# Block transposes on VectorE for a scan's inputs and outputs, with block layouts in DRAM, and another order of the lanes

## The chip, the cores and the metric

The kernel runs on 1 core of one Trainium2 chip. The metric is the device time of one execution in microseconds; runs of one kernel are compared by their median. One execution is also profiled, and that is the trace read here.

## The reference

One layer of a bidirectional hybrid encoder, for a group of 256 tokens ("prompt") and one of 1024 ("sample") with the same weights. Width 2048.

```
hn   = rms_norm(x);  proj = hn @ w_in
xbc, z_ssd, dt_raw, q, k, v, z_att, mq, z_mem = split(proj)
xbc  = silu(centred_dwconv(xbc, conv_w, conv_b))        # 5 taps along the tokens, 1536 channels
xs, B, C = split(xbc, (1024, 256, 256))
y    = ssd_scan(forward) + ssd_scan(backward) + d_skip * xs       # chunks of 128 tokens, 16 heads of 64
o_ssd = rms_norm(y * silu(z_ssd), per group of 512 channels)
o_att = window_attention(q, k, v, sink) * silu(z_att)
o_mem = memory_attention(mq, rms_norm(mem) @ w_mem_kv) * silu(z_mem)
out  = x + concat[o_ssd, o_att, o_mem] @ w_out
```

All in float32. Each large product is made of three float32r matmuls, with both operands split into a high and a low part (names that end in H and L, or wh and wl).

## The kernel before, in words

The 1280 tokens are ten tiles of 128: 0 to 7 are the sample, 8 and 9 the prompt, and they are worked in two groups of five tiles (640 tokens). There are two kinds of weight stage. `block_tok` makes 512 output columns for up to five token tiles, with 16 steps over the input features (three matmuls a tile and step). `block_pair` makes the feature-major outputs (channels on the partitions, tokens along the row) with seven products in place of eight; each unit has 8 steps, GpSimd makes the weight sums (`ws`), ScalarE and VectorE split them (`wh`, `sh`, `wl`, `sl`).

In order of time: the memory's keys and values; `q` for group 1; `seven_stage(1)` (100 to 380 us) with the feature-major part of `w_in` (gates, and the 12 blocks `fc` of 128 convolution channels); `kv` and `q`; `seven_stage(0)` (460 to 714 us); then the token-major stages of `w_in` from 714 us on, beside which the scan and both attentions run; then `w_out`, token-major first (1272 to 1550 us) and by pairs last.

**The convolution.** `conv_work` takes a finished block `u` of 128 channels x 642 columns through five taps and a SiLU, and its `last` stores it in DRAM in `xbc_d`, rows of channels by columns of tokens. Blocks 0 to 7 are x, 8 to 11 are B and C. Its pieces stand in the queue `left` and are taken out a piece at a time between the weight steps.

**The lanes.** In the later stages, what isn't a weight matmul is written as generators in four lanes: ATT (`attn`, `mem_attn`), SSD (`ssd_one`, `ssd_two`), PREP (heads' norms and transposes) and DEC (`decay`). After each weight step `pump` gives every lane some credit and takes steps from lanes that may run. A step yields `wants(tiles, banks, after)`: a small clock model (`Clocks`) holds it back until its tiles should be ready and, if it needs PSUM, until a bank should be free; with `banks` over 0 the tiles must be ready, otherwise they may be 300 ns away. `said` holds what is done. `pump` asks the lanes in a fixed order. `need` and `settle` take steps by force where a later stage can't go on without them: `refill_o(0)` wants `attn` 4, `mem_attn` 4 and `ssd_two` 5.

**The scan.** `ssd_one(t)` goes through the sample's tiles downward from 7 to 0 and then 9 and 8. It loads x, B and C of its tile from `xbc_d`, turns x so that tokens stand on the partitions (`pxs`, four 128x128 transposes on TensorE for each half of 512 channels), copies it out of PSUM (`xs`), and makes the chunk states. `decay(t)` makes the part within the chunk and stores `yp_d`. `ssd_two(t)` goes upward, adds the other direction, multiplies by the gate and takes the norm. The finished y of a tile is turned back one tile later by `turn_ssd`: four transposes on TensorE (`pr`), a copy by ScalarE (`so`), and a store to `oT_d[2 + g]`, where channels stand on the rows and a group's 640 tokens along them.

**Who reads `oT_d`.** `refill_o(0)` loads group 0's outputs as the rows of the token-major `w_out` stages (`fill_direct`, tile `chd`); `seven_load` loads group 1's for the stage by pairs (`raw`, profile names `ra` and `rb_`).

All these DMAs are issued by SyncE, in one queue, with the weight loads (`wraw`).

Of the kernel before, what the change touches and what calls it, by code (L numbers as in the profile page):

```python
# [19 lines left out]
P = 128  # L20
D = 2048
KT = D // P
NT = 10
# [122 lines left out]
def wants(*tiles, banks=0, after=()):  # L146
    return tiles, banks, after
# [3 lines left out]
def hymba_encoder_kernel(  # L151
# [67 lines left out]
    def dram(shape, name):  # L219
        return dr.tile(shape, F32, tag=name, name=name)  # L220

    xbc_d = dram([12, P, NT * P], "xbc_d")
    z_d = [[dram([P, 512], f"z{c}_{t}") for t in range(NT)] for c in range(2)]
    zT_d = [[dram([P, 4, 640], f"zT{c}_{g}") for g in range(2)] for c in range(2)]
    q_d = [dram([P, 512], f"q_{t}") for t in range(NT)]
    mq_d = [dram([P, 512], f"mq_{t}") for t in range(NT)]
    kv_d = [dram([P, 288], f"kv_{t}") for t in range(NT)]
    oT_d = [[dram([P, 4, 640], f"oT{c}_{g}") for g in range(2)] for c in range(4)]
    yp_d = [dram([P, 1024], f"yp_{t}") for t in range(NT)]
    sb_d = [dram([P, 1024], f"sb_{t}") for t in range(NT)]  # L230
    row_d = [[dram([P, 640], f"row{n}{k}") for n in "HL"] for k in range(KT)]
# [1 line left out]
    ac_d = [dram([160, P], f"ac_{g}") for g in range(2)]  # L233
    mr_d = [dram([P, 512], f"mr_{i}") for i in range(4)]
    mv_d = dram([P, 4, 512], "mv_d")

    def turned(out, x):

# [62 lines left out]
    def pump(rates):  # L301

        for i in range(4):
            owed[i] = min(owed[i] + rates[i % 2], DEBT) if lanes[i] else 0.0
        while True:
            i = next((j for j in (ATT, PREP, SSD, DEC) if may(j)), None)
            if i is None:
                return
            owed[i] -= 1
            step(i)  # L310
# [10 lines left out]
    def fill_direct(q, j, src, gain=None, n=640, norm=False):  # L321

        ch = rp.tile([P, 640], F32, tag="ch", name="chd", bufs=CH)[:, :n]
        last_load[0] = S.dma_start(ch, src)
        yield
        h, l = [x[:, :n] for x in new_place(4 * q + j)]
        if norm:
            V.scalar_tensor_tensor(out=ch, in0=ch, scalar=gain, in1=rbc, op0=ALU.mult, op1=ALU.mult)
            gain = None
        if gain is None:  # L330
            A.activation(h, ch, AF.Copy)
            V.tensor_sub(l, ch, h.bitcast(F32))
        else:
            A.activation(h, ch, AF.Copy, scale=gain)
            V.scalar_tensor_tensor(out=l, in0=ch, scalar=gain, in1=h.bitcast(F32), op0=ALU.mult, op1=ALU.subtract)
        yield
# [96 lines left out]
    def conv_work(grp, fc, u):  # L433

        n = 642
        cw = [vec[:, R_CW + k * 12 + fc:R_CW + k * 12 + fc + 1] for k in range(5)]
        c = []

        def first_tap():
            if grp:  # L440
                V.memset(u[:, 384:388], 0.0)
                V.memset(u[:, 644:646], 0.0)
                V.tensor_copy(carry[:, fc, :], u[:, :4])
            else:
                V.memset(u[:, :2], 0.0)
                V.tensor_copy(u[:, 642:646], carry[:, fc, :])
            c.append(ev.tile([P, 650], F32, tag="evt", name="c")[:, :n])
            A.activation(c[0], u[:, :n], AF.Identity, scale=cw[0], bias=vec[:, R_CB + fc:R_CB + fc + 1])

        def tap(k):  # L450
            V.scalar_tensor_tensor(out=c[0], in0=u[:, k:k + n], scalar=cw[k], in1=c[0], op0=ALU.mult, op1=ALU.add)

        def silu():
            A.activation(u[:, :n], c[0], AF.Tanh)

        def last():
            V.scalar_tensor_tensor(out=u[:, :n], in0=u[:, :n], scalar=1.0, in1=c[0], op0=ALU.add, op1=ALU.mult)
            if grp == 0:
                S.dma_start(xbc_d[fc, :, 0:642], u[:, :n])
            else:  # L460
                S.dma_start(xbc_d[fc, :, 642:1024], u[:, :382])
                S.dma_start(xbc_d[fc, :, 1024:1280], u[:, 386:n])
        return [first_tap] + [lambda k=k: tap(k) for k in range(1, 5)] + [silu, last]
# [484 lines left out]
    def ssd_one(t):  # L948
# [5 lines left out]
        xc = []  # L954
        for g in range(2):
            x = wb("xc", shape=(P, 4, P))
            S.dma_start(x, xbc_d[4 * g:4 * g + 4, :, tok].rearrange("f p c -> p f c"))
            xc.append(x)
        yield wants(bc, banks=1, after=prior(t, "weighed"))
        ps = psum("pcb")  # L960
# [10 lines left out]
        said.add(("ssd_one", t, "cb"))  # L971
        xsT = []
        for g in range(2):
            yield wants(xc[g], banks=1, after=prior(t) + (("dt_prep", t // 5 * 5),))
            ps = psum("pxs")
            for j in range(4):
                turned(ps[:, j * P:(j + 1) * P], xc[g][:, j, :])
            xt = mp.tile([P, 512], F32, tag="xs", name="xs", bufs=2)
            V.tensor_copy(xt, ps)
            xsT.append(xt)  # L980
        xs_of[t] = xsT
        yield wants(cb)
# [162 lines left out]
    def turn_ssd(g):  # L1145

        if g in last_y:
            t, y = last_y.pop(g)
            ps = psum("pr")
            for j in range(4):  # L1150
                T.transpose(ps[:, j * P:(j + 1) * P], y[:, j * P:(j + 1) * P], ident)
            o = mp.tile([P, 512], F32, tag="rb", name="so", bufs=RBB)
            A.activation(o, ps, AF.Copy)
            S.dma_start(oT_d[2 + g][t // 5][:, :, t % 5 * P:(t % 5 + 1) * P], hv(o, 4))

    def ssd_two(t):
        first = t in (NS - 1, NT - 1)
        last = t in (0, NS)
        tok = slice(t * P, (t + 1) * P)
        yield wants(after=(("decay", t // NS * NS),))  # L1160
        ss = sm.tile([P, 2], F32, tag="s2", name="yss", bufs=4)
        if not last:
            cc = mp.tile([P, 2, P], F32, tag="btok", name="cc", bufs=1)
            S.dma_start(cc, xbc_d[10:12, :, tok].rearrange("f p c -> p f c"))
        ld = []
        for g in range(2):
            c = slice(g * 512, (g + 1) * 512)

            y = mp.tile([P, 512], F32, tag="ya" if t % 2 else "rf", name="yd", bufs=2)
            S.dma_start(y, yp_d[t][:, c])  # L1170
            z = mp.tile([P, 512], F32, tag="xs", name="zd", bufs=2)
            S.dma_start(z, z_d[g][t])
            st = None
            if not first:
                st = state[:, c] if last else wb("st2")
                S.dma_start(st, sb_d[t][:, c])
            ld.append((y, z, st))
        yield wants(*([last_y["y"][2]] if "y" in last_y else []))
        norm_ssd()
        for g in range(2):  # L1180
            c = slice(g * 512, (g + 1) * 512)
            y, z, st = ld[g]
            yield wants(y, z, *(() if last else (cc, state)), banks=0 if last else 1)
            if not last:
                pf = psum("pyb")
                T.matmul(pf, cc[:, g, :], state[:, c], start=True, stop=True)
                y2 = wb("y3")
                V.tensor_mul(hv(y2), hv(pf), hb(eacs_all[:, t, 8 * g:8 * g + 8], 8, 64))
                V.tensor_add(y, y, y2)
            V.tensor_mul(y, y, z)  # L1190
            if not first and not last:
                V.tensor_mul(hv(state[:, c]), hv(state[:, c]), hb(cd_all[:, t, 8 * g:8 * g + 8], 8, 64))
                V.tensor_add(state[:, c], state[:, c], st)
            yield wants(y)
            A.activation(z, y, AF.Square, scale=0.5, accum_out=ss[:, g:g + 1])
            if g in last_y:
                yield wants(last_y[g][1], banks=1)
                turn_ssd(g)
        yield wants(ss)
        rs = sm.tile([P, 2], F32, tag="s2", name="yrs", bufs=4)  # L1200
        rsqrt(rs, ss, 1.0 / 512, 2)
        G.tensor_scalar(out=rs, in0=rs, scalar1=0.5, scalar2=None, op0=ALU.mult)
        last_y["y"] = t, [x[0] for x in ld], rs
        if first:
            yield wants(rs)
            norm_ssd()
            for g in range(2):
                yield wants(last_y[g][1], banks=1)
                turn_ssd(g)

    seven = {1: (0, 0, 0), 2: (0, 1, 5), 6: (1, 1, 2), 5: (1, 0, 1), 3: (1, 2, 6), 7: (0, 3, 3), 4: (0, 2, 4)}
# [2 lines left out]
    def seven_load(k):  # L1214

        q, j = divmod(k, 4)
        raw[k] = [rp.tile([P, 640], F32, tag="ch", name=n, bufs=CH) for n in ("ra", "rb_")]
        S.dma_start(raw[k][0], oT_d[q][1][:, j, :])
        S.dma_start(raw[k][1], oT_d[2 + q][1][:, j, :])

    def seven_sums(k):
        a, b = raw[k]
# [358 lines left out]
    def refill_o(grp):  # L1581
        def f(q):
            need((attn, mem_attn, ssd_two, ssd_two)[q], [4 if q < 2 else 5])
            return [part(fill_direct, q, j, oT_d[q][grp][:, j, :],
                         gain=None if q < 2 else vec[:, R_SG + 4 * (q - 2) + j:R_SG + 4 * (q - 2) + j + 1])
                    for j in range(4)]
        return f
# [225 lines left out]
    return out  # L1813


W_AT, _o = {}, 0
for _n, _c, _t in _blocks():
    W_AT[_n] = (_o, len(_c), _t)
# [54 lines left out]
```

## Time and profile before

| | |
|---|---|
| three runs | 1776.07, 1778.87, 1780.52 us; median 1778.87 |
| the profiled execution | 1773.83 us, its span 1772.1 us |
| granted TensorE clock | 1.000 |
| tile `pxs` on TensorE | 80 transposes, 782.7 to 1331.8 us |
| tile `pr` on TensorE | 80 transposes, 1161.8 to 1409.9 us |
| DMA, whole span | 313.23 MB in 210993 packets, 21584 of them under 512 B |

Nearly every instruction passes through one helper line (L128), so the groups are told apart by the names of their tiles: `pr<-identr,yd` is what writes `pr` from `identr` and `yd`. PE is TensorE's matmuls, PEld its weight loads, DVE VectorE, ACT ScalarE, POOL GpSimd and SP SyncE. "Idle before" is the time in which the engine stood still ahead of the instructions of a group, and "<-" what ended it. The ends of matmuls are modelled and overlap: what a matmul costs is read from one start to the next.

### The profile page before, as it was taken

To read this page: it belongs to the slowest core of one execution; us is meant where nothing else is said; L and a number is where in the kernel's file an instruction comes from. 1 tells how busy PE (TensorE), PEld (TensorE's weight loads), DVE (VectorE), ACT (ScalarE), POOL (GpSimd) and SP (SyncE) were. 2 spreads that over 40 slices of the span, in tenths; PEclk is the share of its full clock that TensorE was granted. 3 is DMA by queue.
4 is the path that set the end of the run, shared out by engine and by line. 5 is a ranking of instruction groups with operands and counts; after the bars stand their busy time and mean duration, and the time that the engine had idled before them with its cause. 6 is when DMAs were issued, how large, how long until landed. Compare 5 with 4: busy or idle time off the path is not lost.

```text
span 1772.1 us, 30974 instructions
## 1 busy us (share of the span) xinstructions
PE 1755.3 (99%) x10306; PEld 1572.0 (89%) x10306; DVE 1310.9 (74%) x2417; ACT 971.8 (55%) x2181; POOL 683.8 (39%) x1092
## 2 busy tenths in 40 slices
PE   9999999999999999999999999999999999999999
PEld 7889999999899999988788877887788888889999
DVE  5596788989968888797777877678776533766665
ACT  6554555445545444346787666658886532433332
POOL 0026798860478989220110000111200100068775
PEclk9999999999999999999999999999999999999999
DMA  8794454446544333376467766767785734644442
GB/s 293 238 319 175 136 149 148 128 143 194 156 119 145 119 104 106 90 216 208 143 188 249 259 213 192 226 190 230 243 249 161 222 110 147 207 142 147 145 144 77
DMA packets 210993, 313.23 MB, mean 177 GB/s; under 512 B 21584, under 2 KB 84368, under 8 KB 210832
## 3 DMA queue, kind: packets, MB, share of 16 engines
q1 hardware_dynamic: 210688, 311.19, 56.7%
q8 instruction: 81, 1.33, 0.3%
q14 instruction: 80, 0.66, 0.1%
q10 hardware_dynamic: 144, 0.06, 0.0%
HBM read 242.42 MB, written 68.75 MB: 176 GB/s over the span
## 4 chain that ended last, share of the span: by engine, by line
PE 88%; DMA 4%; DVE 3%; ACT 2%; issue 1%; POOL 1%; SPq 0%; ACTq 0%; DVEq 0%; POOLq 0%
PE acc L128 66%; PE accm L128 11%; PE py L128 2%; PE po L128 1%; PE psc L128 1%; PE pst L128 1%; PE pmo L128 1%; PE pms L128 1%; PE ppt L128 1%; DMA wraw<-in_w_in_laid_dram 1%; PE pyf L128 1%; DMA xst<-in_x_prompt_dram 1%; DVE wl L128 1%; PE pyb L128 0%; ACT lg L128 0%
## 5 line engine op out<-in xcount | busy, mean ns | idle before, releaser
L128 PE MATMUL acc<-wh,xH 128*128 128x512 f32 (+1 forms) x1248 | 490.0, 393 | 0.1
L128 DVE TENSOR_TENSOR wl<-wraw,wh 128x512 fp32r<-128x512 f32 (+1 forms) x480 | 355.5, 744 | 172.9 <-ACT wh L128 170.1
L128 PE MATMUL acc<-wl,xH 128*128 128x512 f32 (+1 forms) x1248 | 473.7, 380 | 0.7 <-DVE wl L128 0.5
L128 PE MATMUL acc<-wh,xL 128*128 128x512 f32 (+1 forms) x1248 | 472.1, 378 | 0.0
L128 ACT ACTIVATE wh<-wraw 128x512 fp32r<-128x512 f32 (+1 forms) x480 | 291.5, 613 | 211.6 <-PE acc L128 136.5
L128 POOL TENSOR_TENSOR ws<-wraw 128x128 f32<-128x128 f32 x224 | 156.9, 700 | 365.8 <-DMA wraw<-in_w_in_pairs_dram 163.1
L128 PEld LDWEIGHTS acc<-wl,xH 128*128 128x128 f32 x1248 | 234.7, 188 | 45.1 <-issue 6.5
L128 PEld LDWEIGHTS acc<-wh,xH 128*128 128x128 f32 x1248 | 234.6, 188 | 44.9 <-issue 7.0
L128 PEld LDWEIGHTS acc<-wh,xL 128*128 128x128 f32 x1248 | 234.2, 188 | 44.6 <-issue 1.0
L128 ACT ACTIVATE sh<-ws 128x384 fp32r<-128x384 f32 x224 | 115.5, 522 | 253.3 <-POOL ws L128 126.6
L128 DVE TENSOR_TENSOR sl<-ws,sh 128x384 fp32r<-128x384 f32 x224 | 158.7, 712 | 115.4 <-ACT sh L128 113.9
L128 POOL TENSOR_TENSOR ws<-wraw,ws 128x128 f32<-128x128 f32 x224 | 153.1, 683 | 17.2
L128 POOL TENSOR_TENSOR ws<-ws,wraw 128x128 f32<-128x128 f32 x224 | 154.3, 689 | 0.0
L128 POOL TENSOR_TENSOR wraw<-wraw 128x128 f32<-128x128 f32 x224 | 139.8, 624 | 17.1
L128 PE MATMUL acc<-xH,wl 128*128 128x320 f32 x320 | 100.0, 312 | 1.0 <-DVE wl L128 1.0
L128 PE MATMUL acc<-tH,sl 128*128 128x320 f32 x320 | 98.9, 309 | 0.0
L128 PE MATMUL acc<-xL,wh 128*128 128x320 f32 x320 | 98.9, 309 | 0.0
L128 PE MATMUL accm<-tH,wl 128*128 128x320 f32 x320 | 98.8, 309 | 0.0
L128 PE MATMUL acc<-tH,sh 128*128 128x320 f32 x320 | 98.7, 309 | 0.0
L128 PE MATMUL acc<-xH,wh 128*128 128x320 f32 x320 | 98.7, 309 | 0.0
L128 PE MATMUL accm<-tL,wh 128*128 128x320 f32 x320 | 98.5, 308 | 0.0
L128 PE MATMUL accm<-tH,wh 128*128 128x320 f32 x320 | 98.5, 308 | 0.0
(458 smaller groups left out, 3829.1 us busy)
## 6 DMA issues: line engine op xcount, KB each, us to landing
wraw<-in_w_in_pairs_dram SPq DMA_DIRECT2D x160, 256.0 KB, 2.7
wraw<-in_w_in_laid_dram SPq DMA_DIRECT2D x128, 256.0 KB, 3.6
wraw<-in_w_out_laid_dram SPq DMA_DIRECT2D x64, 256.0 KB, 3.1
wraw<-in_w_out_pairs_dram SPq DMA_DIRECT2D x64, 256.0 KB, 2.9
rf<-ac SPq DMA_DIRECT2D x40, 256.0 KB, 3.8
rb<-ac SPq DMA_DIRECT2D x40, 256.0 KB, 4.2
wraw<-in_w_mem_laid_dram SPq DMA_DIRECT2D x32, 256.0 KB, 4.7
ra<-in_x_turned_dram SPq DMA_DIRECT2D x16, 320.0 KB, 3.8
```

What stands on the lines that cost most here:

```text
L128: r = f(*a, **kw)
```

## The change

- `ssd_one` loads x from a new tensor `x_d`, as blocks of 32 tokens, so that a 32x32 block transpose by VectorE from SBUF to SBUF gives `xs`. The eight transposes on TensorE a tile, their PSUM banks and the copies are gone. 
- A 32x32 block transpose turns within blocks and leaves their places; the places are made good by the layout of `x_d`, by the loads' patterns and by an order of x's channels (`BLOCKED`), by which the columns of `w_in`, the rows of `w_out`, the convolution's weights and the norm's gains are laid out ahead of the launch.
- `conv_work` stores blocks 0 to 7 in `x_d`, in runs of 32 floats, with an extra DMA for the columns at the groups' edge; blocks 8 to 11 go to `xbc_d` as before.
- `turn_ssd` turns y with VectorE's block transpose; TensorE's transposes, the PSUM bank and ScalarE's copy are gone. `oT_d[2]` and `oT_d[3]` are laid out in blocks; `fill_direct` and `seven_load` read them in runs of 32 floats.
- `pump` asks SSD and DEC ahead of ATT and PREP from the time that `mem_attn` 4 is done until `ssd_two` 5 is.

```diff
+    x_d = dram([8, NT * 4, P, 32], "x_d")
...
-    oT_d = [[dram([P, 4, 640], f"oT{c}_{g}") for g in range(2)] for c in range(4)]
+    oT_d = [[dram([P, 4, 640] if c < 2 else [4, 20, P, 32], f"oT{c}_{g}") for g in range(2)] for c in range(4)]
...
+    def blocks(x):
+        return x.rearrange("b p j -> p b j")
+
+    def in_blocks(x):
+        return x.rearrange("p (b j) -> p b j", j=32)
+
+    def turned_blocks(x):
+        return x.rearrange("f a (i q) j -> (a i) f (q j)", q=4)
...
-            i = next((j for j in (ATT, PREP, SSD, DEC) if may(j)), None)
+            late = ("mem_attn", 4) in said and ("ssd_two", 5) not in said
+            i = next((j for j in ((SSD, DEC, ATT, PREP) if late else (ATT, PREP, SSD, DEC)) if may(j)), None)
...
-        last_load[0] = S.dma_start(ch, src)
+        last_load[0] = S.dma_start(in_blocks(ch) if len(src.shape) == 3 else ch, src)
...
-            if grp == 0:
+            if fc < 8:
+                if grp == 0:
+                    S.dma_start(blocks(x_d[fc, 0:20]), in_blocks(u[:, :640]))
+                    S.dma_start(x_d[fc, 20, :, 0:2], u[:, 640:n])
+                else:
+                    S.dma_start(x_d[fc, 20, :, 2:32], u[:, :30])
+                    S.dma_start(blocks(x_d[fc, 21:32]), in_blocks(u[:, 30:382]))
+                    S.dma_start(blocks(x_d[fc, 32:40]), in_blocks(u[:, 386:n]))
+            elif grp == 0:
...
-            S.dma_start(x, xbc_d[4 * g:4 * g + 4, :, tok].rearrange("f p c -> p f c"))
+            S.dma_start(x, turned_blocks(x_d[4 * g:4 * g + 4, 4 * t:4 * t + 4]))
...
-            yield wants(xc[g], banks=1, after=prior(t) + (("dt_prep", t // 5 * 5),))
-            ps = psum("pxs")
-            for j in range(4):
-                turned(ps[:, j * P:(j + 1) * P], xc[g][:, j, :])
+            yield wants(xc[g], after=prior(t) + (("dt_prep", t // 5 * 5),))
             xt = mp.tile([P, 512], F32, tag="xs", name="xs", bufs=2)
-            V.tensor_copy(xt, ps)
+            V.transpose(xt, xc[g].rearrange("p f c -> p (f c)"))
...
-            ps = psum("pr")
-            for j in range(4):
-                T.transpose(ps[:, j * P:(j + 1) * P], y[:, j * P:(j + 1) * P], ident)
             o = mp.tile([P, 512], F32, tag="rb", name="so", bufs=RBB)
-            A.activation(o, ps, AF.Copy)
-            S.dma_start(oT_d[2 + g][t // 5][:, :, t % 5 * P:(t % 5 + 1) * P], hv(o, 4))
+            V.transpose(o, y)
+            S.dma_start(turned_blocks(oT_d[2 + g][t // 5][:, t % 5 * 4:t % 5 * 4 + 4]), hv(o, 4))
...
-                yield wants(last_y[g][1], banks=1)
+                yield wants(last_y[g][1])
...
-        S.dma_start(raw[k][1], oT_d[2 + q][1][:, j, :])
+        S.dma_start(in_blocks(raw[k][1]), blocks(oT_d[2 + q][1][j]))
...
-            return [part(fill_direct, q, j, oT_d[q][grp][:, j, :],
+            return [part(fill_direct, q, j, oT_d[q][grp][:, j, :] if q < 2 else blocks(oT_d[q][grp][j]),
...
+BLOCKED = [128 * f + 32 * q + i for f in range(8) for i in range(32) for q in range(4)]
```

More of the change, by code (lines that the diff above doesn't have):

```diff
@@ L1207, in ssd_two @@
             for g in range(2):
-                yield wants(last_y[g][1], banks=1)
+                yield wants(last_y[g][1])
                 turn_ssd(g)
@@ L1844 @@
     za = _np.arange(C_ZA, C_ZA + 512).reshape(2, 4, 64).transpose(1, 0, 2).reshape(512)
-    c = _np.concatenate([za, _np.arange(C_ZM, C_ZM + 512), _np.arange(C_X, C_X + 1536)]).reshape(10, 256)[list(UNITS)].ravel()
+    c = _np.concatenate([za, _np.arange(C_ZM, C_ZM + 512), C_X + _np.array(BLOCKED), _np.arange(C_X + 1024, C_X + 1536)]).reshape(10, 256)[list(UNITS)].ravel()
     p = w[:, c].reshape(2, 8, P, 10, 2, P)
@@ L1849 @@
     w = _np.asarray(inputs['w_out'])[0]
+    w = _np.concatenate([w[BLOCKED], w[1024:]])
+    inputs['ssd_norm_g'] = _np.asarray(inputs['ssd_norm_g']).ravel()[BLOCKED]
     att = w[1024:1536].reshape(2, 4, 64, D).transpose(1, 0, 2, 3).reshape(512, D)
@@ L1855 @@
     inputs['w_out_pairs'] = _np.stack([w[0, :, :, 0], w[1, :, :, 0], w[1, :, :, 1], w[0, :, :, 1]]).transpose(3, 1, 2, 0, 4).reshape(8, 8, P, 512)
+    for n in ('conv_b', 'conv_w'):
+        inputs[n] = _np.take(_np.asarray(inputs[n]), BLOCKED + list(range(1024, 1536)), axis=-1)
     inputs['vecs'] = _np.concatenate([_np.asarray(inputs[n]).reshape(-1, P) for n in
```

## The prediction

> **What bounds the kernel now.** I read the totals first, then the chain that ended last.
>
> ```profile
> span 1772.1 us, 30974 instructions
> PE 1755.3 (99%) x10306; PEld 1572.0 (89%) x10306; DVE 1310.9 (74%) x2417; ACT 971.8 (55%) x2181; POOL 683.8 (39%) x1092
> ...
> PE 88%; DMA 4%; DVE 3%; ACT 2%; issue 1%; POOL 1%; SPq 0%; ACTq 0%; DVEq 0%; POOLq 0%
> ```
>
> PE is busy for 1755.3 of 1772.1 us and carries 88% of the chain. An instruction taken off PE shortens the span unless what replaces it makes PE wait. VectorE is next, so I cut the span by stage to see where it has room. The columns are the stretch, its length, then the busy time of PE, PEld, DVE, ACT and POOL, the clock, the DMA share and GB/s.
>
> ```profile
> 380.00:460.00 80.00, 80.00 (x500) 74.64 (x499) 73.33 (x127) 39.51 (x72) 16.26 (x17) 1.00 0.56 170
> 460.00:714.00 254.00, 253.71 (x1676) 249.26 (x1675) 213.24 (x312) 123.27 (x228) 208.22 (x311) 1.00 0.41 123
> 760.00:1160.00 400.00, 392.43 (x2136) 321.25 (x2134) 309.16 (x705) 272.81 (x741) 44.83 (x78) 1.00 0.66 207
> 1160.00:1290.00 130.00, 128.38 (x698) 100.34 (x696) 103.83 (x234) 96.20 (x244) 22.39 (x48) 1.00 0.73 226
> 1460.00:1560.00 100.00, 100.00 (x443) 82.80 (x442) 57.39 (x97) 40.33 (x67) 4.59 (x6) 1.00 0.56 169
> ```
>
> The edits to the scan fall in 760 to 1450 us. PE idles there for 7.57 + 1.62 us, no more, and VectorE has room: 77% busy, then 80%. The row of 380 to 460 shows VectorE at 73.33/80 = 92% while PE waits for nothing.
>
> **The transposes that leave PE.** Two groups of four transposes go, each twenty times. A matmul's duration overlaps its neighbour's, so the price is read from starts.
>
> ```profile
> 1400.42 0.39 PE L128 MATMUL acc<-wh,xL 128*128 128x512 f32 x1
> 1400.65 0.60 PE L128 MATMUL pr<-identr,yd 128*128 128x128 f32 x4
> 1401.01 0.48 PE L128 MATMUL acc<-wh,xH 128*128 128x512 f32 x1
> 1401.32 0.39 PE L128 MATMUL acc<-wl,xH 128*128 128x512 f32 x1
> 1401.55 0.39 PE L128 MATMUL acc<-wh,xL 128*128 128x512 f32 x1
> ...
> 1331.35 0.40 PE L128 MATMUL acc<-wh,xH 128*128 128x512 f32 x1
> 1331.59 0.45 PE L128 MATMUL pxs<-identr,xc 128*128 128x128 f32 x4
> 1331.88 0.47 PE L128 MATMUL acc<-wl,xH 128*128 128x512 f32 x1
> 1332.18 0.40 PE L128 MATMUL acc<-wh,xL 128*128 128x512 f32 x1
> ```
>
> Undisturbed, a 512-column matmul starts 0.23 us after the one before (1401.32 to 1401.55). From 1400.42 to 1401.55 stand three of them and one group of pr: 1.13 - 3 x 0.23 = 0.44 us for pr. From 1331.35 to 1332.18 stand two and one group of pxs: 0.83 - 2 x 0.23 = 0.37 us. The counts come from the groups by line:
>
> ```profile
> L128 DVE COPY xs<-pxs 128x512 f32<-128x512 f32 x20 | 13.3, 681 | 0.3 <-PE pxs L128 0.3
> L128 PE MATMUL pr<-identr,yd 128*128 128x128 f32 x80 | 11.9, 275 | 0.3 <-DVE y L128 0.3
> L128 ACT ACTIVATE so<-pr 128x512 f32<-128x512 f32 x20 | 11.6, 592 | 6.7 <-PE pr L128 6.6
> L128 PE MATMUL pxs<-identr,xc 128*128 128x128 f32 x80 | 9.2, 247 | 1.2 <-DMA xc<-xbc_d 0.8 <-DVE nm L128 0.4
> L128 DVE TENSOR_SCALAR yd<-yd,yrs 128x512 f32<-128x512 f32 x20 | 9.0, 483 | 12.5 <-POOL yrs L128 12.5
> L128 DVE RECIPROCAL dtw<-dtw 128x160 f32<-128x160 f32 x6 | 6.9, 1146 | 0.1
> ```
>
> So 20 x 0.44 + 20 x 0.37 = 16.2 us leave PE, about 7.4 us by xs and 8.8 by so. PE's own waits ahead of them (1.2 + 0.3 us) may go too; I count them at zero, because the data still has to come before the next step of the scan, and keep 0 to 1.5 us for the range.
>
> **VectorE takes them over.** The copy of xs out of PSUM (681 ns) becomes a 32x32 block transpose, in its place. The copy of so on ScalarE (592 ns, twenty of them, off the path: 96.20 of 130 us busy) becomes another one on VectorE. No row shows this operation. The nearest is the copy of the same 128x512 elements, 681 ns, and I take it. The ends are the 483 ns of the scaling, and RECIPROCAL's rate: 1146 ns for 160 elements, 3.7 us for 512. At 681 ns xs costs VectorE nothing new and so adds 20 x 0.68 = 13.6 us. By stage, so's rows are (length, ScalarE busy):
>
> ```profile
> 1160.00:1290.00 130.00, 9.35 (x16) 1.00 0.73 226
> ```
>
> Sixteen fall in one stage. There VectorE stands at 103.83 + 10.9 = 114.7 us in a stage of 130 - 16 x 0.44 = 123 us: 93%, against the 92% that PE was seen to bear. I charge 1 us of new waits. VectorE's block of work would make the weights' low part late, and PE behind it.
>
> The Trainium skill, in "VectorE: DVE Perf Modes", section "The three transpose paths", gives 311 ns for a 128x128 VectorE transpose in bf16. Four of them would be 1.24 us (an estimate by that page), by which that stage would gain nothing and the sum would be 14.2 - 7 = 7.2 us; no run shown so far has such an instruction.
>
> VectorE now also waits for the load of xc itself, where PE did. That wait came to 0.8 us in twenty loads, so the loads land ahead of their use, and I charge nothing; behind such a wait stand the weights' splits.
>
> **The smaller pieces in DRAM.** Loads of xc and stores of so keep runs of 512 B (four blocks of 32 floats side by side). Stores of x and loads of oT go from rows to runs of 128 B: 640 columns are 20 x 128 = 2560 pieces, 160 on each of 16 engines. What a piece costs comes from three short stretches of the DMA queue (packets, MB, share of 16 engines): 0.6 us at 783.62 us with loads of 128 B, 1 us at 1403.4 with a store of 512 B, 1 us at 1112.4 with 2 KB.
>
> ```profile
> q1 hardware_dynamic: 220, 0.03, 27.8%
> ...
> q1 hardware_dynamic: 478, 0.24, 89.2%
> ...
> q1 hardware_dynamic: 137, 0.25, 64.7%
> ```
>
> They give 0.278 x 16 x 600/220 = 12.1 ns, 29.9 ns and 75.6 ns a packet (the last mixed with some tiny ones). A blocked transfer then holds the engines for 160 x 12.1 = 1.94 us, where eight rows of 2.5 KB to an engine held them for about 8 x 75.6 x 1.25 = 0.76: 1.2 us more. This happens in three places.
>
> First, 16 stores of x in the two stages of convolution, with 16 more DMAs in all for the edges of 2 and 30 columns. SP has time to issue them, at about half a microsecond each (the stores of oT below, in ns):
>
> ```profile
> SPq L128 <- DVE wl L128: 581.1, 324, 6.8
> ...
> PE acc L128 <- DVE wl L128: 1.5, 4, 0.5
> ...
> L128 SPq DMA_DIRECT2D oT<-so x20: 513/519/1430, 1163.3 to 1412.2; - x20
> L128 SPq DMA_DIRECT2D oT<-moT x10: 518/519/620, 1103.3 to 1446.1; - x10
> L128 SPq DMA_DIRECT2D ra<-oT x8: 320/326/384, 1384.1 to 1541.0; - x8
> ```
>
> It stands 581.1 us waiting for free weight buffers. Weights queued behind a store come 1.2 us late; a step lasts 254/80 = 3.2 us, loads run two steps ahead, and all of PE's waits for split weights are 1.5 us in the whole span. A 128 B store is shown nowhere: I take the load's 12.1 ns, keep 29.9 (a piece of 512 B) as the other end, and charge 1 us for all 16.
>
> Second, eight loads of chd in 1160 to 1290, which may come 1.2 us later, asked for two steps ahead where a step has 15 matmuls of 0.23 us and the lanes' work besides: nothing. Third, eight loads of the last stage:
>
> ```profile
> L128 SPq DMA_DIRECT2D rb__17947<-oT x1: 432/432/432, 1417.4 to 1417.4; - x1
> L128 ACT ACTIVATE rb__17947<-rb__17947,vec x1: 817/817/817, 1492.5 to 1492.5; 128x640 f32<-128x640 f32 x1
> ```
>
> The first is issued 75 us ahead of its use. Later ones are nearer, but PE is busy for 100.00 of 100 us there with ScalarE at 40 and VectorE at 57: nothing.
>
> **The order of the lanes.** From the fifth tile of mem_attn to ssd_two(5) the scan's lanes step ahead of attention. It moves PE's, ACT's, VectorE's, POOL's and SP's instructions alike (loads of yp, z and sb come earlier, attn(5)'s exponentials on POOL later) and adds none. It can gain no more than the 1.62 us that PE idles in 1160 to 1290. It can lose by crowding VectorE, since a scan tile is heavy there: that is in the rival below. Attention ends later, with room: its last output goes to DRAM at 1446.1 us, and the last stage's loads of it (ra, above) run until 1541.0. I count zero. The channel order of weights and vectors is settled ahead of the launch.
>
> **The sum.** 16.2 - 1 - 1 = 14.2 us. The profiled execution took 1773.83 us (span 1772.1 and 1.7 around it), 5.0 below the median of 1778.87. It would take 1759.6; on the median, 1764.7.
>
> **The rivals.**
> VectorE becomes the bound (0.17). With a transpose at two copies (1.36 us), 103.83 + 16 x 1.36 = 125.6 us meet a stage of 123, and the reordered scan crowds them more. It decides from (0.92 x 123 - 103.83)/16 = 0.58 us of added work a tile half if 92% is all that PE bears. Then the gain of that stage (7 us) is lost: 1778.87 - 7.2 = 1772. Against it: waiting attention steps leave VectorE free.
>
> Small stores hold up the weights (0.15; the side that ends slower). Place: the two convolution stages. With some 4 us of cover (two steps of 3.2, less the splitting), a store of 160 pieces at p ns costs PE 160p - 0.76 - 4 us. Sixteen of them eat 14.2 us at p = 35 ns; at 40 ns PE loses 26 us: 1790. For it: no store of this size is shown, and POOL has only 18% to spare there (208.22 of 254). Against it: 12.1 ns for the load, and 29.9 for a store of four times the size.
> The Trainium skill, "DMA: Bandwidth & Descriptors", section "Specifications", says that below 512 B the engine reads, modifies and writes. The 12.1 ns of the loads do not show it. Were each store doubled by that rule (24 ns, an estimate), the formula stays below zero and the sum stands.
>
> The scan's chain gets shorter (0.10): without a PSUM bank and a turn on PE its steps come sooner, and half of the 9.2 us that PE idles in 760 to 1290 goes as well, with no new waits: 1778.87 - 16.2 - 4.6 = 1758.
>
> **How the numbers follow.** The forecast has 0.58: 1764, alone 1759 to 1769. Under 0.3% (5.3 us) this measurement can't tell a change. Faster: 0.58 + 0.10 + 0.10 of VectorE's case = 0.78. Same: 0.07 of it and 0.03 of milder stores = 0.10. Slower: 0.12. The range goes from 1755 (the shorter chain, and 3 us as the runs scatter) to 1776, past VectorE's case; about 0.15 lies above and 0.05 below.
>
> **What would show it.** No rows of pr and pxs on PE; PE's busy time 14 to 21 us lower; so and xs as VectorE rows near 0.68 us; at most some microseconds of "PE acc <- DVE wl" in 1160 to 1290. If the small stores hurt, POOL waits longer for w_in_pairs in 100 to 714 us and these stages lengthen. A transpose over 1 us, or convolution stages that grow by more than a few microseconds, would make the prediction wrong.

## The result, and the profile after

| | before | after |
|---|---|---|
| median of four runs | 1777.88 us (1776.07 to 1780.52) | 1764.65 us (1764.20 to 1766.60) |
| the profiled execution, its span | 1773.83, 1772.1 us | 1764.86, 1763.1 us |

The ratio of after to before is 0.9934, with an interval of 0.9921 to 0.9946: 13.2 us faster, where 1764 us had been forecast. By the profiled executions alone it is 9.0 us (1773.83 - 1764.86), since that run of the kernel before lay 4 us under its median. The changed kernel's totals, its chain and its DMA packets:

```profile
span 1763.1 us, 30613 instructions
PE 1743.8 (99%) x10146; PEld 1558.8 (88%) x10146; DVE 1323.4 (75%) x2437; ACT 962.8 (55%) x2161; POOL 683.0 (39%) x1092
...
PE 82%; DMA 6%; DVE 4%; POOL 3%; ACT 2%; issue 2%; SPq 0%; DVEq 0%; POOLq 0%; ACTq 0%
...
DMA packets 289070, 313.19 MB, mean 178 GB/s; under 512 B 104784, under 2 KB 165520, under 8 KB 288912
```

PE has 160 matmuls fewer and is busy for 11.5 us less; outside them the span holds 19.3 us instead of 16.8. So of 11.5 us that PE no longer works, 2.5 us came back as idle time, and 9.0 us are the span's. VectorE is busy for 12.5 us more, ScalarE for 9.0 less, and nearly five times as many packets are under 512 B (21584 before). PE's share of the chain fell from 88% to 82%: the end now leans a little more on transfers and VectorE. The stages that the prediction cut out and, as the first row, the other convolution stage, in the same columns (length, busy time of PE, PEld, DVE, ACT, POOL, clock, DMA share, GB/s):

```profile
100.00:380.00 280.00, 278.38 (x1775) 268.54 (x1774) 230.60 (x366) 141.37 (x274) 213.78 (x321) 1.00 0.56 168
460.00:714.00 254.00, 253.66 (x1664) 247.85 (x1663) 212.56 (x314) 123.58 (x229) 206.13 (x308) 1.00 0.44 124
760.00:1160.00 400.00, 393.41 (x2092) 323.44 (x2091) 308.80 (x699) 270.27 (x728) 43.10 (x75) 1.00 0.66 206
1160.00:1290.00 130.00, 127.18 (x609) 99.70 (x608) 108.57 (x219) 73.58 (x173) 20.79 (x41) 1.00 0.81 236
1240.00:1340.00 100.00, 95.86 (x489) 73.81 (x488) 79.47 (x179) 73.29 (x197) 12.94 (x27) 1.00 0.86 238
1460.00:1560.00 100.00, 100.00 (x480) 83.83 (x479) 64.10 (x114) 50.87 (x96) 11.14 (x16) 1.00 0.55 146
```

The convolution stage of 460 to 714 still has PE without a gap; in that of 100 to 380 PE idles 1.6 us. The fifth row is a stretch that the prediction did not cut out, the start of the token-major output stages with the end of the scan beside them: PE idles 4.1 us there, with the DMA engines at 0.86. The kernel before had these rows for the first and the fifth:

```profile
100.00:380.00 280.00, 279.34 (x1787) 270.35 (x1787) 230.94 (x368) 142.30 (x275) 216.49 (x323) 1.00 0.55 169
1240.00:1340.00 100.00, 98.70 (x548) 78.14 (x547) 74.55 (x181) 82.00 (x228) 12.88 (x29) 1.00 0.77 237
```

It idled 0.7 us in the first, and in the other 1.3 us, with a share of 0.77. The tile `xs` of the changed kernel (duration in ns: least, median, most; then VectorE's idle time ahead of it, in us and times, and what ended it):

```profile
L128 DVE STREAM_TRANSPOSE xs<-xc x20: 670/706/715, 783.0 to 1337.0; 128x512 f32<-128x512 f32 x20
...
  DMA xc<-x_d: 7.5, 5
```

And the tile `so`:

```profile
L128 DVE STREAM_TRANSPOSE so<-yd x20: 667/704/716, 1168.8 to 1402.9; 128x512 f32<-128x512 f32 x20
```

A block transpose of 128x512 float32 takes 0.70 us, beside the 0.681 us taken. Now PE's waits, the largest of them with their sum, their number and the longest:

```profile
PE psc L128 <- ACT pT L128: 3.4, 4, 1.5
PE acc L128 <- DVE wl L128: 2.3, 6, 0.6
PE psc L128 <- ACT cb L128: 1.7, 3, 0.7
PE pmq L128 <- DVE moT L128: 1.4, 1, 1.4
```

None is new and large: many waits of about a microsecond in other places than before.

### The profile page after: what moved, and what is told of

The parts are those of the page before. It is cut to its first block, busy times and chain, and to the rows that moved or that the text cites. A ratio compares the mean times of both kernels' runs of the same rounds, so it can differ in the third digit from the quotient of the medians.

```text
span 1763.1 us, 30613 instructions
## 1 busy us (share of the span) xinstructions
PE 1743.8 (99%) x10146; PEld 1558.8 (88%) x10146; DVE 1323.4 (75%) x2437; ACT 962.8 (55%) x2161; POOL 683.0 (39%) x1092
## 4 chain that ended last, share of the span: by engine, by line
PE 82%; DMA 6%; DVE 4%; POOL 3%; ACT 2%; issue 2%; SPq 0%; DVEq 0%; POOLq 0%; ACTq 0%
PE acc L128 63%; PE accm L128 10%; POOL ws L128 2%; PE py L128 2%; PE psc L128 1%; PE po L128 1%; PE pst L128 1%; DMA rb<-ac 1%; DVE wl L128 1%; DMA rf<-ac 1%; PE pmo L128 1%; PE ppt L128 1%; PE pyb L128 1%; PE pms L128 1%; DMA xc<-x_d 1%
## 5 line engine op out<-in xcount | busy, mean ns | idle before, releaser
L128 POOL TENSOR_TENSOR ws<-wraw,ws 128x128 f32<-128x128 f32 x224 | 153.2, 684 | 17.4
```

The source lines that it names most:

```text
L128: r = f(*a, **kw)
```

## The experiments

The letters in the expectations are these. P: the 16.2 us of starts that PE loses carry the gain, less what new waits take back. O: the order of the lanes is worth several microseconds. O': in e1 and e2, the new order costs time; in e14 and e15, it is worth several microseconds by itself. S: the small stores of x hold up the weights of the convolution stages. V: VectorE is crowded. W: one or more waits move elsewhere. D: loads in pieces of 128 B keep the DMA engines so busy that weights come late at the start of the output stages. C: any change of the plan by which `pump` lets steps go moves the time by several microseconds, whatever it is meant to do. T: the plan with 155 is simply a better one. Each ratio is to runs of the kernel before on the same chip.

### Parts of the change

**The old order with both transposes.**

```diff
-            late = ("mem_attn", 4) in said and ("ssd_two", 5) not in said
-            i = next((j for j in ((SSD, DEC, ATT, PREP) if late else (ATT, PREP, SSD, DEC)) if may(j)), None)
+            i = next((j for j in (ATT, PREP, SSD, DEC) if may(j)), None)
```

> The changed kernel with the old fixed order of the lanes. Theory P (TensorE's 16.2 us carry the gain, the order moves work and removes none): within 3 us of the changed kernel, 1762 to 1768 us. Rival O (the order is what keeps the crowded scan from costing time): 1770 us or more, with more waits of PE between 1160 and 1290 us. Rival O' (scan first crowds VectorE and takes part of the gain back): 1760 us or less.

Measured: 1776.49 us, ratio 0.9992 (0.998 to 1.0005). Without the order at most about 1 us is left of the 13. Its page:

```profile
span 1774.6 us, 30595 instructions
PE 1746.4 (98%) x10146; PEld 1560.6 (88%) x10146; DVE 1321.4 (74%) x2437; ACT 963.3 (54%) x2161; POOL 685.6 (39%) x1092
```

PE's work did fall, by 8.9 us; but 28.2 us of the span now lie outside it, 11.4 more than before. Its largest wait of PE is a new one:

```profile
PE acc L128 <- ACT wh L128: 5.5, 2, 2.9
```

Its windows give the place, first the stretch of the output stages, then the middle of it by five microseconds:

```profile
1240.00:1340.00 100.00, 90.62 (x449) 68.18 (x448) 75.93 (x168) 69.14 (x181) 15.34 (x30) 0.97 0.85 225
...
1295.00:1300.00 5.00, 2.06 (x17) 1.34 (x14) 2.30 (x5) 3.11 (x8) 0.13 (x1) 1.00 0.91 194
1300.00:1305.00 5.00, 5.00 (x18) 4.06 (x17) 5.00 (x17) 5.00 (x15) 0.19 (x1) 0.66 0.76 194
1305.00:1310.00 5.00, 3.85 (x18) 2.87 (x16) 3.67 (x8) 2.04 (x5) 0.78 (x1) 1.00 0.98 189
1310.00:1315.00 5.00, 3.56 (x10) 2.85 (x11) 2.33 (x4) 4.21 (x12) 0.00 (x0) 0.66 1.00 229
```

And its chain has this piece there (start, length, what, in us):

```profile
1292.93 5.54 DMA wraw<-in_w_out_laid_dram
```

PE stands for 2.9 us in 1295 to 1300 because ScalarE's split `wh` is late; the split waits for a weight load that was issued at 1292.93 and took 5.54 us. SyncE's queue had stood behind waits of other DMAs, and the engines were 0.91 busy, so both a late issue and a slow landing may be in it: weight loads of the kernel before land in 4.1 us there (1240 to 1340, median). A second loss follows: the granted clock falls to 0.66 over the next five microseconds, and again after the next gap.

**The order alone.** The two lines above, the other way round, in the kernel before.

> The kernel before with the new order alone. Theory P: the same as before within 3 us (1775 to 1781). Rival O: the order pays by itself, 1772 us or less. Rival O': slower than before by more than 3 us.

Measured: 1782.52 us, 1.003 (1.0018 to 1.0042): 4.8 us slower, against what P expected, and as O' of this run had it. So the order is not worth 12 us as such.

**xs alone, and so alone**, both in the old order. xs alone is this part of the change and the stores of x (`so` stays on TensorE):

```diff
+            S.dma_start(x, turned_blocks(x_d[4 * g:4 * g + 4, 4 * t:4 * t + 4]))
...
+            V.transpose(xt, xc[g].rearrange("p f c -> p (f c)"))
```

> xs alone (x in blocks, turned by VectorE), normed output as before, old order. Theory P: 20 x 0.37 = 7.4 us off PE, less what the small stores cost (1 to 3 us): 4 to 7 us under the kernel before. Rival S (the small stores of x hold up weights): no gain or a loss, and the two convolution stages end later by as much as is missing. Rival W (VectorE now waits for loads of xc): no gain, with the convolution stages unchanged and the stretch 760 to 1160 us as long as before.

Measured: 1777.94 us, 1.000 (0.999 to 1.0009). so alone is `turn_ssd` by VectorE and the blocked `oT_d`, with no small store of x:

```diff
+            V.transpose(o, y)
+            S.dma_start(turned_blocks(oT_d[2 + g][t // 5][:, t % 5 * 4:t % 5 * 4 + 4]), hv(o, 4))
```

> The normed output alone (turned by VectorE, its DRAM tensors in blocks), xs as before, old order. Theory P: 20 x 0.44 = 8.8 us off PE, no small stores (its stores keep runs of 512 B), 0.7 us a tile half more on VectorE: 7 to 9 us under the kernel before. Rival V (VectorE becomes the bound in 1160 to 1290 us): 0 to 4 us under it.

Measured: 1772.3 us, 0.9967 (0.9955 to 0.9979). The first has no row of `chd` in pieces, the second has. Yet the second is the better one, and in 1240 to 1340 its PE is busy for 99.31 us with the DMA share at 0.86:

```profile
1240.00:1340.00 100.00, 99.31 (x530) 77.77 (x528) 80.10 (x189) 79.45 (x219) 13.39 (x29) 1.00 0.86 236
```

A high share by itself does not make weights late. The parts do not add up either: +0.2 and -5.4 apart, -1.3 together. Both fall short of P, 4 to 7 us and 7 to 9. PE's busy time in their profiled executions is 1754.8 and 1750.1 us, only 0.5 and 5.2 less than before, at mean clocks of 0.998 and 0.999.

S is not quite out by xs alone. In its profiled execution, which lay 6.7 us above its median, PE idles 4.1 us in 100 to 380 and 0.8 us in 460 to 714 (0.7 and 0.3 before). But so alone, without any small store of x, idles 2.3 and 1.0 us there, so at most part of that can be the stores. Where else xs alone loses its gain was not traced.

### The loads in pieces of 128 B

In these two kernels the blocked loads of `chd` and `rb_` read the same bytes as rows of 2.5 KB; the blocks are then not put back in their places, so the scan's part of the output is left out of place.

```diff
-        S.dma_start(in_blocks(raw[k][1]), blocks(oT_d[2 + q][1][j]))
+        S.dma_start(raw[k][1], as_rows(oT_d[2 + q][1][j]))
...
-            return [part(fill_direct, q, j, oT_d[q][grp][:, j, :] if q < 2 else blocks(oT_d[q][grp][j]),
+            return [part(fill_direct, q, j, oT_d[q][grp][:, j, :] if q < 2 else as_rows(oT_d[q][grp][j]),
```

> The changed kernel with the old order, and with the loads of the scan's outputs (chd and the second of seven_load's pair) as rows of 2.5 KB from the same regions of DRAM: the output is wrong in the part that comes from the scan, as the blocks are not put back in place. Theory D (with the old order, eight loads in 2560 pieces each meet the start of the output stages, where the DMA engines are 80% busy, and make weights late): at least half of the 12 us between the old and the new order come back, 1770 us or less, with no wait of PE on split weights between 1285 and 1315 us. Rival O (the lanes' order by itself, whatever the loads): 1774 to 1779 us as with blocks.

> The changed kernel (new order) with the same loads as rows, the scan's part of the output wrong for the same reason. Theory D: the loads still cost something, 1758 to 1763 us. Rival O: 1764 to 1766 us, unchanged. If the order had nothing to do with the loads, this and the old order with rows differ by some 12 us as before.

Measured: the old order with rows 1770.39 us, 0.996 (0.9948 to 0.9971); the new order with rows 1763.87 us, 0.9925 (0.9913 to 0.9937). The stretch of the output stages, in the first and in the second:

```profile
1240.00:1340.00 100.00, 95.33 (x499) 72.88 (x499) 80.90 (x180) 73.81 (x198) 14.73 (x30) 1.00 0.77 243
```

```profile
1240.00:1340.00 100.00, 96.85 (x506) 75.78 (x505) 81.81 (x186) 76.22 (x205) 13.60 (x28) 1.00 0.76 242
```

The share returns to the 0.77 of before, the wait of PE for `wh` is gone, and the clock is whole. In the old order the time falls by 6.1 us (1776.49 to 1770.39, on two chips whose runs of the kernel before lie 0.8 us apart), in the new order by 0.8 us, which is inside its scatter. Each lies just above the range that D gave (1770, and 1758 to 1763).

But the edit changes more than the size of the pieces: the order in which SyncE issues its transfers changes with it. These are its issues in the old order around the first weight load after 1255 us, then the same with rows (start, length, in us):

```profile
1281.57 3.40 SPq L128 DMA_DIRECT2D xc<-x_d  x2
...
1286.03 0.43 SPq L128 DMA_DIRECT2D chd<-oT  x1
1290.64 1.64 SPq L128 DMA_DIRECT2D oT<-so  x2
...
1292.93 0.62 SPq L128 DMA_DIRECT2D wraw<-in_w_out_laid_dram  x1
```

```profile
1284.92 0.98 SPq L128 DMA_DIRECT2D xc<-x_d  x2
1285.95 0.50 SPq L128 DMA_DIRECT2D wraw<-in_w_out_laid_dram  x1
```

With rows the weights stand right behind the loads of `xc`; with pieces they stand behind two stores of `so` as well, ahead of which SyncE issues nothing from 1286.5 to 1290.6, and are issued 7 us later. So the pair does not tell the small pieces from the place in the queue. D's late weights are seen in this plan; that the small pieces make them late is not shown, and in the new order the edit changes next to nothing.

### The plan itself

The clock model, which decides when a lane's step may go, plans a VectorE operation at a fixed 150 ns and 1.05 ns an element. The next six kernels change that 150 and nothing else by hand, so that each version of the kernel is seen under three plans.

```diff
         if e == "DVE":
-            return 150 + 1.05 * n
+            return 155 + 1.05 * n
```

The changed kernel, and the transposes in the old order, planned with 155:

> The changed kernel with VectorE's fixed cost in the lanes' clock model at 155 ns in place of 150: no work is changed, but steps are released a little otherwise and the order of the instructions changes from 760 us on. Theories P and D: within 3 us of the changed kernel. Rival C (what order the planner happens on decides several microseconds, so that single differences of this size can't be put down to a mechanism): more than 4 us away.

> The old order with the same 155 ns. Theory D: the loads still meet the weights, within 4 us of the old order's 1776.5 us. Rival C: more than 5 us away, towards the changed kernel's time.

The kernel before planned with 155 and with 145, and the other two with 145:

> The kernel before with one number of its planner changed: an operation of VectorE is planned with 155 instead of 150 fixed. No instruction is added or taken away, the order of some is. Theory C (the plan alone decides several us, in every version): this one too leaves 1777 us by 3 to 6 us, to either side. Theory T (the plan with 155 is simply a better one): 1770 to 1773, and then nothing of the 1770.64 of both transposes in the old order under this plan is owed to the transposes. Theory P (the transposes' 16.2 us of PE are gained under any plan, less what new waits take back): 1776 to 1784, that is 6 to 13 us over the two changed versions of this plan, 1772.74 and 1770.64.

> The kernel before, planned with 145 instead of 150. It is the third plan of the kernel before. Theory C: within 6 us of 1777 on either side. Theory P: 6 to 13 us over the mean of the two changed versions planned with 145. If the three plans of the kernel before lie within 2 us of each other, it is the changed kernels alone that depend on their plan.

> The changed kernel, planned with 145 instead of 150. Theory O' (the order of the lanes is worth several us by itself): 1762 to 1767, and 5 us or more under the old order planned with 145. Theory C (what the order did at 150 was a plan that escaped a wait): 1766 to 1774, within 4 us of the old order, or over it. Theory D (loads in pieces of 128 B make weights late at the start of the output stages, where the plan puts them close): where it is over 1769, the rows show a wait of PE for the first weights of that stage between 1280 and 1320 us and a granted clock under 1.00 in 1240 to 1340.

> Both transposes by VectorE with the lanes in the old order, planned with 145 instead of 150. With it there are three plans of each of three versions (before; transposes in the old order; transposes in the new order). Theory P: 6 to 13 us under the kernel before planned with 145; PE's busy time some 13 us lower, as in each pair so far. Theory O': over the new order of the same plan by 5 us or more. Theory C: 1766 to 1776, on either side of the new order. Theory D as for the new order: over 1769, a late weight at the start of the output stages and a clock under 1.00.

Measured, all nine (median of the runs; in brackets PE's busy time in the profiled execution, and the rest of its span):

| plan | before | both transposes, old order | both transposes, new order |
|---|---|---|---|
| 150 | 1777.88 (1755.3, 16.8) | 1776.49 (1746.4, 28.2) | 1764.65 (1743.8, 19.3) |
| 155 | 1789.41 (1762.8, 26.6) | 1770.64 (1745.3, 24.5) | 1772.74 (1746.0, 24.0) |
| 145 | 1788.39 (1759.6, 23.4) | 1766.88 (1742.2, 23.0) | 1769.45 (1745.8, 25.4) |
| mean | 1785.2 (1759.2, 22.3) | 1771.3 (1744.6, 25.2) | 1768.9 (1745.2, 22.9) |

The ratios to the kernel before under its own plan: 1.0064 (1.005 to 1.0077) and 1.0062 (1.0044 to 1.0079) for the kernel before with 155 and 145; 0.9972 (0.9963 to 0.9981) and 0.9960 (0.9948 to 0.9972) for the new order; 0.9967 (0.9955 to 0.9979) and 0.9933 (0.9921 to 0.9946) for the old. The columns come from several chips, whose medians of the kernel before lie between 1776.97 and 1778.36 us.

Three things follow. First, C: five nanoseconds in a planning constant move one version by 5 to 12 us, either way (the kernel before by +11.5 and +10.5, the new order by +8.1 and +4.8, the old by -5.9 and -9.6). Second, P: read along the rows, PE's busy time drops in each of the six pairs (by 8.9, 17.5 and 17.4 us in the old order, by 11.5, 16.8 and 13.8 in the new), and the medians by 1.4 to 21.5 us, 13.9 us in the mean for the transposes alone. T falls with that: the kernel before is slower with 155. In the two new plans the gains, 16.7 to 21.5 us, are above the 6 to 13 that P expected there. Third, O' falls: from the old order to the new it is -11.8, +2.1 and +2.6 us, a mean of -2.4 that three plans can't tell from zero. What the order did at 150 was to lead to a plan in which the start of the output stages stalls less.

D was tested once more by these. The two with 155 show late weights in the stretch where D put them. The changed kernel planned with 155, its largest wait of PE and the stretch of the output stages:

```profile
PE acc L128 <- ACT wh L128: 4.8, 1, 4.8
```

```profile
1240.00:1340.00 100.00, 89.92 (x448) 68.10 (x447) 77.65 (x179) 71.50 (x188) 14.41 (x28) 0.95 0.88 237
```

The transposes in the old order planned with 155, the same two views:

```profile
PE acc L128 <- ACT wh L128: 7.8, 2, 7.3
```

```profile
1240.00:1340.00 100.00, 89.13 (x431) 66.78 (x430) 81.43 (x178) 63.93 (x170) 15.00 (x30) 0.95 0.89 248
```

Yet in the changed kernel planned with 155 the chain there is this:

```profile
1293.45 4.03 DMA oT<-so
1297.48 0.02 issue
1297.50 2.42 SPq L128
1299.92 0.05 issue
1299.97 4.32 DMA wraw<-in_w_out_laid_dram
```

The weight load landed in 4.32 us, hardly more than the 4.1 us of the kernel before. It came late because it was issued late, behind an issue that stood until a store of `so` had landed. Whether small pieces had a share in that is not shown.

And the new order planned with 145 is over 1769 us without any wait for `wh`, against what D expected of it. It pays through other waits of PE in 1160 to 1340, and its row of the stretch follows them:

```profile
PE po L128 <- ACT pT L128: 1.9, 1, 1.9
PE psc L128 <- DVE oT L128: 1.9, 1, 1.9
PE psc L128 <- ACT cb L128: 1.7, 1, 1.7
PE pq L128 <- DVE nm L128: 1.6, 1, 1.6
```

```profile
1240.00:1340.00 100.00, 92.86 (x458) 71.35 (x459) 73.11 (x165) 64.87 (x173) 10.50 (x25) 0.97 0.84 224
```

The kernel before planned with 155 stalls in that stretch as well, with its loads in whole rows: 3.4 us in two waits of PE for VectorE's `nm`, a DMA share of 0.78, and the clock at 0.98:

```profile
PE psc L128 <- DVE nm L128: 3.4, 2, 1.7
```

```profile
1240.00:1340.00 100.00, 93.48 (x486) 70.32 (x485) 76.27 (x184) 76.83 (x207) 15.66 (x35) 0.98 0.78 245
```

So the stretch from 1160 to 1340, where the scan, the attentions' ends and the first output weights meet, is the place where plans differ most. A late weight load is one way to stall there, and no more than one; how much of it the small pieces cause stays open. Which plan stalls how was not derived from anything ahead of a run; that stays open. No version tried beats the changed kernel by more than the scatter of its runs.

## Why the prediction was right, and where it was not

**PE's starts (16.2 us).** Right in size, by the mean. It expected PE's busy time 14 to 21 us lower; the pair shown gave 11.5, outside, and the three plans give 14.6 (old order) and 14.0 (new) in the mean. Part of PE's busy time is a lower granted clock: in the mean of the trace, with 150, 155 and 145, it is 1.000, 0.998 and 0.999 before, 0.997, 0.997 and 0.999 in the old order, 0.999, 0.997 and 0.998 in the new. An estimate that takes (1 - clock) x span off each busy time gives drops of 13 to 19 us, about 17 and 16 in the mean; the clock is given to 0.001, so it is good to a microsecond or two. By that the transposes' price was right, and the pair shown lost part of it to the clock.

**VectorE's transpose at a copy's price.** Right: 0.70 us against 0.681, and 12.5 us more of busy time against 13.6. In 1160 to 1290 VectorE is busy for 108.57 us of 130, 84%, where 93% had been worked out: less of its other work falls in that stretch (219 instructions with the 16 new ones, where there were 234), and in the old order too (221, 106.06 us). PE's waits for `wl` are 2.3 us in the whole span, 0.8 more than before, beside 1 us charged. The rival in which VectorE becomes the bound is refuted here. The Trainium skill's 311 ns for a block of 128x128 in bf16 ("VectorE: DVE Perf Modes", "The three transpose paths") would have made four of them 1.24 us, an estimate by that page; the trace has 0.70 us for all four in float32, so the sum of 7.2 us by that page was too low.

**The small stores.** They cost what the loads cost. Two stretches of 1 us of the changed kernel's DMA queue, the first at 697 us with stores of x in 128 B alone, the second at 1403.6 with a store of `so` in 512 B (packets, MB, share of 16 engines; the share counts a packet's whole time where it begins, and can pass 100%):

```profile
q1 hardware_dynamic: 1682, 0.22, 136.7%
...
q1 hardware_dynamic: 409, 0.21, 75.5%
```

They give 1.367 x 16 x 1000/1682 = 13.0 ns and 29.5 ns a packet. The prediction took 12.1 and kept 29.9 as the far end; its rival needed 35. The Trainium skill's rule of a read, modification and write below 512 B ("DMA: Bandwidth & Descriptors", "Specifications") does not show in the time of these packets. The convolution stage of 460 to 714 lost nothing: PE is busy for 253.66 of 254 us there, as before. In that of 100 to 380 PE idles 1.0 us more, which is what was charged; as so alone, without these stores, idles more still, it can't be put down to them.

**Loads of `xc`, charged at nothing.** VectorE waits 7.5 us for five of the twenty. All five lie between 990 and 1125 us, and of PE's waits for `wl` only 0.4 us fall in 714 to 1160. So through late splits next to nothing reached PE, though the waits themselves were underrated; what they did through other work of VectorE was not separated.

**The step that failed: "The order of the lanes", with its "It can gain no more than the 1.62 us that PE idles in 1160 to 1290".** The bound was read from the trace of before, which has the old order and the old work. With the transposes gone, PE idles 28.2 us in the old order, 9.4 of them in 1240 to 1340, and 19.3 us in the new, 4.1 of them there: 8.9 us less, and 11.8 us by the medians, where 1.62 was to be the most. The zero that was counted stands better: over the three plans the order's worth can't be told from nothing. The same step should have asked what any change of the plan costs. The sum of 14.2 us is near the mean over plans (13.9 in the old order, 16.3 in the new), but one draw of it scatters from 1.4 to 21.5.

**Loads of `chd`, "nothing".** Not safe as a rule. With rows in their place the old order is 6.1 us faster and the new 0.8 us, with another order of SyncE's issues as well. The argument looked at one load, asked for two steps ahead; it left out that weights stand in the same queue behind it, and behind all that it shares the queue with.

**The agreement.** On the profiled execution the sum gave 1759.6 us, and 1764.86 was measured, 5.3 us over; on the median 1764.7 and 1764.65. The second agreement is to a good part luck: both kernels are the best of their three plans, and under the other two plans the gain was 16.7 and 18.9 us, not 13.2.

## What to carry to other kernels

Where one planner or queue order places all work, an edit is measured together with a new plan; run each version under two or three plans that differ in a constant without meaning before a few microseconds are put down to an edit. Read PE's busy time and PE's idle time apart: the first comes nearer to what the edit is worth, and here it fell in every pair, while the second shows the draw. But the first isn't free of the plan either: the same 10306 matmuls of the kernel before were busy for 1755.3, 1762.8 and 1759.6 us under three plans, in part at a lower clock. And before a difference is put down to the size of a transfer, see whether the edit has also changed its place in the queue. A bound on a gain that is read from idle time before holds only as long as the other parts of the change make no idle time of their own.

## What the runs showed of the hardware

A short stall of PE can come with a second loss. In the changed kernel PE waits once for 1.4 us in 1136 to 1139 (for VectorE's `moT`), and the granted clock then falls to about half for 3.4 us:

```profile
1136.00:1139.00 3.00, 1.64 (x15) 1.50 (x15) 2.10 (x7) 0.48 (x2) 1.26 (x2) 1.00 0.53 154
1139.00:1142.40 3.40, 3.40 (x12) 2.72 (x12) 2.62 (x5) 1.56 (x4) 0.00 (x0) 0.54 0.57 190
```

At a clock of 0.54, 3.4 us lose 1.6 us, more than the wait itself. It doesn't follow each time: the kernel before has a wait of 2.3 us (`py`, for ScalarE's `mpT`) at 1095 us, a clock of 1.00 behind it, and a mean of 1.000. The Trainium skill, "TensorE: Matmul & The Clock Gate", section "Part 1: The HAM clock gate", lets the clock fall after an idle window of about 3.4 us; here gaps well under that were enough, so the measurement differs from it.
